# A pool of its own for the second layer's modulation with eight load tiles, the squares of the first norm through PSUM, and transfers for the keys and queries

## The chip, the cores and the metric

The kernel runs on one core of a Trainium2 chip. The engines are named as in the profile: PE (TensorE matmul; PEld is its weight load), DVE (VectorE), ACT (ScalarE), POOL (GpSimd) and SP (SyncE), whose queue issues every DMA of this kernel. The metric is the device time of one execution in microseconds.

## The reference

A small diffusion step of two layers on 128 context tokens and 1024 latent tokens of width 1024. Each layer has a token mixer and a convolutional FFN, both with a modulated RMS norm in front and a gated residual behind.

```python
mc = split(sc @ w_mod[i] + b_mod[i], 6); ml = split(sl @ w_mod[i] + b_mod[i], 6)   # modulation, 2 vectors
hc = rmsnorm(xc, norm_mix[i]) * (1 + mc[1]) + mc[0]       # rmsnorm: x * rsqrt(mean(x*x) + EPS) * g
# layer 0: q, k, v, p = h @ w_in; q, k normed per head; neighbourhood attention of 8 heads
#          (context keys in one softmax with the neighbourhood), pooling of p; concatenation @ w_out
# layer 1: conformer convolution module
xc = xc + mc[2] * yc
hc = rmsnorm(xc, norm_ffn[i]) * (1 + mc[4]) + mc[3]
xc = xc + mc[5] * conv_ffn(hc, ...)                       # @ w_in, conv of 3, silu(a) * g, @ w_out
```

## The kernel before, in words

Everything is feature-major: a tile has 128 features on the partitions and the 1154 columns of the tokens (128 context, a gap of 2, 1024 latent) on the free axis; the residual x is eight such tiles (k = 0 to 7). A float32 product is made of three products of a split pair: `hi` is the value rounded to fp32r (ACT), `lo` the rest (POOL or DVE), and PE does hi*hi, hi*lo, lo*hi.

The work in order of time:

- **The start** (`start0`, L457 to L530). SP loads constants, the eight x, the parameters, then 16 tiles of modulation weights (`mraw`, 512 KB each) with two weight tiles of V (`wraw`) between them. ACT squares each x into an SBUF tile (`sq`, tag `prob`, two buffers); PE sums each square over the partitions with 9 fp32 matmuls of one column (L484), 72 in all, into `ms`. DVE and POOL make the reciprocal root (`rsv`, `rsr`, L368 and L371), PE spreads it over the partitions (`rb`, L490), ACT copies it out (`rs`). The modulation comes in four quarters: eight matmuls (`modps`, L502), a copy (`modev`), four small matmuls (`modt`, L508), then `md` and `g` on DVE. DVE and ACT then make `hhi` and `hlo` of two k per quarter (L521, L524, L525), and PE starts the projection of V (`vps`, L606 to L609) with them.
- **The projections and the attention.** `project_qk` makes the queries and keys of a pair of heads. `split_half` (L664) prepares them for one head b of a pair: of 128 partitions, 64 (`own`) hold the rounded keys `ks` and the other 64 (`oth`) the same again, copied by DVE (L680); `km` gets the rest of the keys (POOL, L681); `qs` gets the rounded queries and, in `oth`, their rest (DVE, L687 and L688); `qm` gets a copy of the rounded queries from POOL (L691). `qm` and `km` are one tile each for head 0 and head 1 of a pair, used again by each of the four pairs, so there are eight halves. The scores (L697, L698) read all four.
- **The output projection** (`out_tiles`) in two parts of the tokens, then the FFN of layer 0, layer 1's convolution and FFN. Beside the output projection and layer 0's FFN, DVE computes the modulation of layer 1 (`mod_beside`, L309): for each of three groups, 32 loads of 128x512 (`mraw`, three buffers, 256 KB each) are multiplied by two scalars into eight accumulators (`modacc`, in tiles of the pool `cv`), and PE sums them over the partitions (L330). The generators are pulled at fixed places (`MS` = 4 loads per tile of the first output projection, `MO` and `MI` in the FFN).

Tiles come from pools with a fixed number of buffers, and the order of each engine's instructions is set by a list scheduler from priorities and modelled times. SP issues DMAs in its order too: one that waits holds up those behind it.

Of the kernel before, what the change touches and what calls it, by code (L numbers as in the profile page):

```python
# [9 lines left out]
F32 = mybir.dt.float32  # L10
F32R = mybir.dt.float32r
AF = mybir.ActivationFunctionType
ALU = mybir.AluOpType
# [6 lines left out]
P = 128  # L20
D = 1024
KT = D // P
# [4 lines left out]
T = L0 + NLAT  # L27
# [90 lines left out]
UW = 692  # L118
# [70 lines left out]
class Kern:  # L189
# [116 lines left out]
        self.mod_spread(l, m, ps, ev, *(last or (psp, tag)))  # L306
        yield

    def mod_beside(self, l, m, wp, ap, tag, ev):  # L309

        nc = self.nc
        accs = [ap.tile([P, UW], F32, tag=tag, name=self.nm("modacc"))[:, :512] for _ in range(8)]
        for k in range(KT):
            for u in range(2):
                for x in range(2):
                    rv = wp.tile([P, 512], F32, tag="mraw", name=self.nm("mraw"), bufs=3)
                    o = u * 1024 + x * 512
                    nc.sync.dma_start(rv, self.i["wmod"][l, m, k, :, o:o + 512])
                    for s in range(2):
                        acc, c = accs[4 * s + 2 * u + x], self.sc[:, k, s:s + 1]  # L320
                        if k == 0:
                            i = nc.vector.tensor_scalar(acc, rv, c, None, op0=ALU.mult)
                        else:
                            i = nc.vector.scalar_tensor_tensor(acc, rv, c, acc, op0=ALU.mult, op1=ALU.add)  # L324
                        self.tc.keep_in_program_order(i)
                    yield
        ps = self.psa.tile([P, 512], F32, tag="aux", name=self.nm("modps"))
        for s in range(2):
            for g in range(4):
                nc.tensor.matmul(ps[32 * g:32 * g + 32, :], self.one[:, 1 - s:33 - s], accs[4 * s + g],  # L330
                                 start=s == 0, stop=s == 1)
        yield
        self.mod_spread(l, m, ps, ev, self.psa, "aux")
        yield
# [122 lines left out]
    def start0(self, up, hp, ap, evac):  # L457


        nc = self.nc  # L460
        mm = nc.tensor.matmul
        xs, raws, wv = [], [], []
        nc.sync.dma_start(self.consts, self.i["consts"])
        for k in range(KT):
            x = up.tile([P, TS], F32, tag="u", name=f"x0_{k}")
            nc.sync.dma_start(x[:, :T], self.i["x"][k])
            xs.append(x[:, :T])
        nc.sync.dma_start(self.params, self.i["params"])
        nc.scalar.activation(self.sc[:, :, 0:2], self.par("cc").rearrange("p (a b) -> p a b", b=2), AF.Silu)
        nc.vector.tensor_scalar(self.qg8, self.par("qg", 0), DH ** -0.5, None, op0=ALU.mult)  # L470
        for i in range(16):
            raw = hp.tile([P, T], F32, tag="h", name=self.nm("mraw"))
            nc.sync.dma_start(raw[:, :1024], self.i["wmod0"][i])
            raws.append(raw)
            if i in (3, 7):
                wv.append(self.wload(self.i["wv"][i // 4]))
        st = [tok0(j) for j in range(9)]
        ms = self.psa.tile([P, 512], F32, tag="aux", name=self.nm("ms"))
        for k in range(KT):
            sq = ap.tile([P, 2, 640], F32, tag="prob", name=self.nm("sq"), bufs=2)  # L480
            sq = sq.rearrange("p a b -> p (a b)")[:, :T]
            nc.scalar.activation(sq, xs[k], AF.Square)
            for j, o in enumerate(st):
                mm(ms[:, j:j + 1], sq[:, o:o + P], self.cst("on"), start=k + j == 0, stop=k == KT - 1 and j == 8)  # L484
        r = self.rsqrt(ms[:, :9], 9)
        rb = self.psm.tile([P, 3, 512], F32, tag="mm3", name=self.nm("rb"))
        for j in range(9):
            c = 0 if j < 3 else j // 3
            n = L0 if j == 0 else P
            mm(rb[:, c, st[j] - CH[c][0]:st[j] - CH[c][0] + n],  # L490
               r[:, j:j + 1].to_broadcast([P, P]), self.cst("id")[:, :n], start=True, stop=True)
        rs = up.tile([P, TS], F32, tag="u", name=self.nm("rs"))
        for pv, sv in self.row3(rb, rs):
            nc.scalar.activation(sv, pv, AF.Copy)
        hhi, hlo = [], []

        def quarters():
            for j in range(4):
                ps = self.psa.tile([P, 512], F32, tag="aux", name=self.nm("modps"))
                for k in range(KT):  # L500
                    g = 32 * (k % 4)
                    mm(ps[g:g + 32, :], self.sc[:, k, :], raws[4 * j + k // 2][:, (k % 2) * 512:(k % 2) * 512 + 512],  # L502
                       start=k < 4, stop=k >= 4)
                ev = evac()
                nc.vector.tensor_copy(ev, ps)
                mt = self.psa.tile([P, 512], F32, tag="aux", name=self.nm("modt"))
                for x in range(4):
                    mm(mt[:, 2 * x:2 * x + 2], ev[:, x * P:(x + 1) * P], self.cst("sl2"), start=True, stop=True)  # L508
                md = self.cp.tile([P, 2, 2, 2], F32, name=self.nm("md"))
                nc.vector.tensor_tensor(md, mt[:, 0:8].rearrange("p (a k s) -> p a k s", a=2, k=2),  # L510
                                        self.par("bm0")[:, :16].rearrange("p (a k) -> p a k", a=2)
                                        [:, :, 2 * j:2 * j + 2, None].to_broadcast([P, 2, 2, 2]), op=ALU.add)
                g = self.cp.tile([P, 2, 2], F32, name=self.nm("g0"))
                nc.vector.scalar_tensor_tensor(g, md[:, 1], 1.0, self.par("nm0")[:, 2 * j:2 * j + 2, None]
                                               .to_broadcast([P, 2, 2]), op0=ALU.add, op1=ALU.mult)
                for x in range(2):
                    t = xs[2 * j + x]
                    hi = hp.tile([P, T], F32R, tag="h", name=self.nm("hhi"))
                    lo = hp.tile([P, T], F32R, tag="h", name=self.nm("hlo"))
                    for s, a, b in ((0, 0, L0), (1, L0, T)):  # L520
                        nc.vector.scalar_tensor_tensor(t[:, a:b], rs[:, a:b], g[:, x, s:s + 1], t[:, a:b],  # L521
                                                       op0=ALU.mult, op1=ALU.mult)
                    for s, a, b in ((0, 0, L0), (1, L0, T)):
                        nc.scalar.activation(hi[:, a:b], t[:, a:b], AF.Identity, bias=md[:, 0, x, s:s + 1], scale=1.0)  # L524
                        nc.vector.scalar_tensor_tensor(lo[:, a:b], t[:, a:b], md[:, 0, x, s:s + 1],  # L525
                                                       hi[:, a:b].bitcast(F32), op0=ALU.add, op1=ALU.subtract)
                    hhi.append(hi)
                    hlo.append(lo)
                yield
        return hhi, hlo, quarters(), wv  # L530
# [133 lines left out]
    def split_half(self, q, k, b, new, res):  # L664


        nc = self.nc
# [4 lines left out]
        def blk(t):  # L672
            return t.rearrange("p (g r c) -> p r g c", g=4, c=16)

        own = slice(64 * b, 64 * b + 64)
        oth = slice(64 - 64 * b, 128 - 64 * b)
        ks = new("ks")
        nc.scalar.activation(ks[own, :], k[own, :T], AF.Copy)
        yield
        nc.vector.tensor_copy(ks[oth, :], k[own, :T])  # L680
        nc.gpsimd.tensor_tensor(self.km[b][own, :], k[own, :T], ks[own, :].bitcast(F32), op=ALU.subtract)  # L681
        yield
        qs = new("qs")
# [4 lines left out]
        nc.vector.tensor_tensor(blk(qs[oth, L0:T]), lat(q[own, L0:T]), blk(qs[own, L0:T]).bitcast(F32),  # L688
                                op=ALU.subtract)
        for o, e in ((0, NCTX), (L0, T)):  # L690
            nc.gpsimd.tensor_copy(self.qm[b][own, o:e], qs[own, o:e])  # L691
        res[b] = (qs, ks)
        yield

# [547 lines left out]
    def trunk(self):  # L1242
        tc, nc, I, cp = self.tc, self.nc, self.i, self.cp
# [10 lines left out]
        with ExitStack() as st:  # L1254
            pool = lambda n, b, **kw: st.enter_context(tc.tile_pool(name=n, bufs=b, reuse_waits="tile", **kw))
# [7 lines left out]
            ft = pool("ft", 4, side="right")  # L1263
            self.fp = pool("fp", 3, side="right")
            hB = pool("hB", 16)
            nt = pool("nt", 3)
            sp = self.sp = pool("cv", 12)
            self.tw = 664
            xs = []
            for k in range(KT):  # L1270
# [8 lines left out]
            for part, Hc in ((OA, mkA()), (OB, mkB(OB.c0))):  # L1279
                Hc.order = order  # L1280
                tiles = {}
                for k in order:
# [5 lines left out]
                                            op=ALU.subtract)  # L1288
# [4 lines left out]
                if part is OA:  # L1293
                    for k in range(KT):
                        nc.sync.dma_start(xs[k], I["x"][k])
            mods = [self.mod_beside(1, m, nt, sp, "s", lambda: nt.tile([P, self.tw], F32, tag="ft", name=self.nm("modev")))
                    for m in range(3)]
            for _ in self.out_tiles(OA, I["woab"], cat[OA], xs, self.mod(0, 2), 0, 664, first=3):
                self.pull(mods, MS)
# [12 lines left out]
            for o in self.ffn(0, FA0, xs, HA, self.mod(0, 5), 0, 662, ft, None):  # L1312
                self.tick(MO if o else MI)
            self.flush(self.bg)


            gm1 = self.gain(1, 1, "nm1")
# [2 lines left out]
            accs = []  # L1320
# [30 lines left out]
            accs = []  # L1351
# [145 lines left out]
```

## Time and profile before

| | us |
|---|---|
| median of 3 runs | 2718.06 (2717.0 to 2720.67) |
| profiled execution | 2718.41 |
| its span | 2716.6 |
| PE busy | 2635.2 (97%) |
| DVE busy | 1605.9 (59%) |
| POOL busy | 1260.9 (46%) |
| ACT busy | 1122.9 (41%) |
| moved by DMA | 341.17 MB |

The span is what the profiler recorded; 1.8 us of the execution's own time lie around it. An engine counts as busy while an instruction is on it, also where that instruction waits inside for a port, and PE is busy too where it works at half its rate or on matmuls of one column. So a busy share says where there is no room left, not that the work there is needed.

### The profile page before, as it was taken

Reading aid. Unit: us, or ns where it says so; the run is one execution under the profiler, and the core shown is the slowest. Engines: PE = TensorE matmul, PEld = TensorE weight load, DVE = VectorE, ACT = ScalarE, POOL = GpSimd, SP = SyncE. Lnnn points to the kernel's source line nnn. Section 1 sums busy time; section 2 is a strip of 40 time slices with the busy share of each in tenths; the row PEclk is TensorE's granted clock in tenths of the full one; section 3 lists DMA queues with packets and bytes.
Section 4 is the critical chain, followed back from the end, with each engine's and each line's share of the span. In section 5 each row is a group of like instructions: output and inputs, shape, how many; then the busy total and the mean of one; then the engine's idle time right before and its main releaser. Section 6 shows DMA issues by size and latency. Waiting matters only on the chain.

```text
span 2716.6 us, 38806 instructions
## 1 busy us (share of the span) xinstructions
PE 2635.2 (97%) x15108; PEld 2379.8 (88%) x15108; DVE 1605.9 (59%) x2456; ACT 1122.9 (41%) x1743; POOL 1260.9 (46%) x752
## 2 busy tenths in 40 slices
PE   8999998889999999999999999999999999999999
PEld 6688887688999999988998789989999999888887
DVE  2236777575476757663997854369974334444444
ACT  3325766525422222245555363555324323433332
POOL 1323444146433232225555353699756544655553
PEclk9999998999999999999999999999999999999999
DMA  7622214364446555544434553232222222433232
GB/s 266 198 76 69 56 53 131 92 223 146 145 150 202 175 174 192 193 147 156 142 133 144 178 179 116 85 88 77 70 74 70 77 85 71 125 93 93 93 95 92
DMA packets 137815, 341.17 MB, mean 126 GB/s; under 512 B 45728, under 2 KB 50976, under 8 KB 137632
## 3 DMA queue, kind: packets, MB, share of 16 engines
q1 hardware_dynamic: 137632, 338.69, 38.8%
q8 instruction: 120, 1.97, 0.3%
q14 instruction: 63, 0.52, 0.1%
HBM read 291.97 MB, written 46.67 MB: 125 GB/s over the span
## 4 chain that ended last, share of the span: by engine, by line
PE 80%; DVE 12%; DMA 3%; ACT 3%; issue 1%; POOL 1%; SPq 0%; POOLq 0%; DVEq 0%; ACTq 0%
PE mm L264 14%; PE mm L266 14%; PE mm L268 14%; PE mn L264 7%; PE mn L266 7%; PE mn L268 7%; DVE modacc L324 2%; DVE dacc L992 2%; PE mm L454 2%; DVE x L437 2%; PE O L884 1%; PE ms L484 1%; PE tp L852 1%; PE qps L634 1%; PE qps L636 1%
## 5 line engine op out<-in xcount | busy, mean ns | idle before, releaser
L254 POOL TENSOR_TENSOR wlo<-wraw,whi 128x1024 fp32r<-128x1024 f32 x280 | 686.0, 2455 | 926.1 <-ACT whi L252 792.6
L252 ACT ACTIVATE whi<-wraw 128x1024 fp32r<-128x1024 f32 x348 | 364.7, 1057 | 770.4 <-PE mm L266 404.5
L264 PE MATMUL mm<-h,whi 128*128 128x332 f32 (+6 forms) x2208 | 559.0, 324 | 11.5 <-DVE x L437 11.5
L268 PE MATMUL mm<-h,wlo 128*128 128x332 f32 (+6 forms) x2208 | 560.5, 324 | 0.4 <-POOL wlo L254 0.3
L266 PE MATMUL mm<-h,whi 128*128 128x332 f32 (+6 forms) x2208 | 559.5, 324 | 0.0
L264 PEld LDWEIGHTS mm<-h,whi 128*128 128x128 f32 x2208 | 383.0, 189 | 25.9 <-issue 12.8
L268 PEld LDWEIGHTS mm<-h,wlo 128*128 128x128 f32 x2208 | 381.3, 189 | 12.4 <-POOL wlo L254 0.9
L266 PEld LDWEIGHTS mm<-h,whi 128*128 128x128 f32 x2208 | 380.0, 189 | 10.4
L992 DVE SCALAR_TENSOR_TENSOR dacc<-u,params,dacc 128x661 f32<-128x661 f32 (+1 forms) x344 | 285.4, 830 | 7.7
L437 DVE SCALAR_TENSOR_TENSOR x<-mm,mod,x 128x128 f32<-128x128 f32 (+7 forms) x408 | 210.4, 561 | 128.3 <-PE mm L268 126.4
L264 PE MATMUL mn<-h,whi 128*128 128x494 f32 (+1 forms) x672 | 262.6, 391 | 3.2 <-DVE x L437 3.2
L266 PE MATMUL mn<-h,whi 128*128 128x494 f32 (+1 forms) x672 | 262.2, 390 | 0.0
L268 PE MATMUL mn<-h,wlo 128*128 128x494 f32 (+1 forms) x672 | 260.6, 390 | 0.0
L1088 DVE SCALAR_TENSOR_TENSOR facc<-mm,params,facc 128x663 f32<-128x663 f32 (+3 forms) x92 | 82.1, 892 | 275.3 <-ACT facc L1087 275.2
L1088 DVE SCALAR_TENSOR_TENSOR facc<-mn,params,facc 128x493 f32<-128x493 f32 (+1 forms) x84 | 62.0, 738 | 219.2 <-ACT facc L1087 219.1
L264 PE MATMUL mm<-fh,whi 128*128 128x332 f32 (+2 forms) x720 | 172.0, 318 | 15.0 <-DVE x L437 13.1
L268 PE MATMUL mm<-fh,wlo 128*128 128x332 f32 (+2 forms) x720 | 170.2, 316 | 0.0
L266 PE MATMUL mm<-fl,whi 128*128 128x332 f32 (+2 forms) x720 | 170.0, 316 | 0.0
L974 POOL TENSOR_TENSOR acc<-acc,tap 128x508 f32<-128x508 f32 (+1 forms) x104 | 151.2, 1457 | 37.1 <-ACT tap L973 31.2
L324 DVE SCALAR_TENSOR_TENSOR modacc<-mraw,sc,modacc 128x512 f32<-128x512 f32 x168 | 158.4, 992 | 0.1
L1100 POOL TENSOR_TENSOR facc<-facc,facc 128x494 f32<-128x494 f32 (+2 forms) x66 | 91.2, 1381 | 144.9 <-DVE facc L1090 136.8
L437 DVE SCALAR_TENSOR_TENSOR x<-mn,mod,x 128x510 f32<-128x510 f32 (+1 forms) x168 | 120.5, 737 | 63.7 <-PE mn L268 62.9
(227 smaller groups left out, 4520.5 us busy)
## 6 DMA issues: line engine op xcount, KB each, us to landing
wraw<-in_fi_dram SPq DMA_DIRECT2D x176, 512.0 KB
wraw<-in_fo_dram SPq DMA_DIRECT2D x88, 512.0 KB
mraw<-in_wmod_dram SPq DMA_DIRECT2D x48, 512.0 KB
mraw<-in_wmod_dram SPq DMA_DIRECT2D x96, 256.0 KB
wraw<-in_pw_dram SPq DMA_DIRECT2D x48, 512.0 KB
lowi<-wlo SPq DMA_DIRECT2D x44, 512.0 KB
wlo<-lowi SPq DMA_DIRECT2D x44, 512.0 KB
lowo<-wlo SPq DMA_DIRECT2D x22, 512.0 KB
```

The source lines that it names most:

```text
L252: nc.scalar.activation(hi, raw, AF.Copy)
L254: (eng or nc.gpsimd).tensor_tensor(lo, raw, hi.bitcast(F32), op=ALU.subtract)
L264: mm(pv, whi, xhi[:, a:b], start=start, stop=False)
L266: mm(pv, whi, xlo[:, a:b], start=False, stop=False)
L268: mm(pv, wlo, xhi[:, a:b], start=False, stop=stop)
L324: i = nc.vector.scalar_tensor_tensor(acc, rv, c, acc, op0=ALU.mult, op1=ALU.add)
L437: nc.vector.scalar_tensor_tensor(xd[:, a:b], pv, gate[:, d, st:st + 1], xd[:, a:b], op0=ALU.mult, op1=ALU.add)
L454: mm(ps[:, c, :n], w[:, s], x[k][:, o:o + n], start=a, stop=b)
L974: nc.gpsimd.tensor_tensor(acc[:, :n], acc[:, :n], p[:, :n], op=ALU.add)
L992: nc.vector.scalar_tensor_tensor(acc[:, :n] if t == NCK - 1 else pacc, u[:, t:t + n], wk(i, t), acc[:, :n] if t == side else pacc, op0=ALU ...
L1088: nc.vector.scalar_tensor_tensor(acc[:, 1:W], part.ps(ps, 0, W - 1), w(0), acc[:, 1:W], op0=ALU.mult, op1=ALU.add)
L1100: (nc.gpsimd if side or part.n == 1 else nc.vector).tensor_tensor(a[:, :W], a[:, :W], g[:, :W], op=ALU.mult)
```

## The change

Four edits:

- In `start0` the squares of k = 1 to 7 go to PSUM tiles (`mm3`), and DVE adds them to the first square in SBUF (L485 of the new kernel); PE then sums over the partitions once, with 9 matmuls instead of 72 (L488).
- In `split_half` the copy of the rounded keys is a DMA from `own` to `oth` instead of a DVE cast, and the copies of the rounded queries to `qm` are DMAs instead of POOL copies. Each of the eight halves gets one DMA for the keys (64 partitions of 1154 columns) and two for the queries (128 and 1024 columns), 24 in all, issued by SP.
- `mod_beside` has a pool `mp` with eight buffers for the loads and eight for the accumulators.
- That pool is closed after layer 0's first FFN part, and the pool `cv` is opened behind it in its place.

```diff
-        accs = [ap.tile([P, UW], F32, tag=tag, name=self.nm("modacc"))[:, :512] for _ in range(8)]
+        accs = [mp.tile([P, 512], F32, tag="macc", name=self.nm("modacc")) for _ in range(8)]
...
-                    rv = wp.tile([P, 512], F32, tag="mraw", name=self.nm("mraw"), bufs=3)
+                    rv = mp.tile([P, 512], F32, tag="mraw", name=self.nm("mraw"))
...
-        ms = self.psa.tile([P, 512], F32, tag="aux", name=self.nm("ms"))
-        for k in range(KT):
-            sq = ap.tile([P, 2, 640], F32, tag="prob", name=self.nm("sq"), bufs=2)
+        acc = ap.tile([P, 2, 640], F32, tag="prob", name=self.nm("sq"), bufs=2)
+        acc = acc.rearrange("p a b -> p (a b)")[:, :T]
+        nc.scalar.activation(acc, xs[0], AF.Square)
+        for k in range(1, KT):
+            sq = self.psm.tile([P, 3, 512], F32, tag="mm3", name=self.nm("sq"))
             sq = sq.rearrange("p a b -> p (a b)")[:, :T]
             nc.scalar.activation(sq, xs[k], AF.Square)
-            for j, o in enumerate(st):
-                mm(ms[:, j:j + 1], sq[:, o:o + P], self.cst("on"), start=k + j == 0, stop=k == KT - 1 and j == 8)
+            nc.vector.tensor_tensor(acc, acc, sq, op=ALU.add)
+        ms = self.psa.tile([P, 512], F32, tag="aux", name=self.nm("ms"))
+        for j, o in enumerate(st):
+            mm(ms[:, j:j + 1], acc[:, o:o + P], self.cst("on"), start=True, stop=True)
...
-        nc.vector.tensor_copy(ks[oth, :], k[own, :T])
+        nc.sync.dma_start(ks[oth, :].bitcast(F32), ks[own, :].bitcast(F32))
...
-            nc.gpsimd.tensor_copy(self.qm[b][own, o:e], qs[own, o:e])
+            nc.sync.dma_start(self.qm[b][own, o:e].bitcast(F32), qs[own, o:e].bitcast(F32))
...
-            sp = self.sp = pool("cv", 12)
+            beside = ExitStack()
+            mp = beside.enter_context(tc.tile_pool(name="mp", bufs=8, reuse_waits="tile"))
...
-            mods = [self.mod_beside(1, m, nt, sp, "s", lambda: nt.tile([P, self.tw], F32, tag="ft", name=self.nm("modev")))
+            mods = [self.mod_beside(1, m, mp, lambda: nt.tile([P, self.tw], F32, tag="ft", name=self.nm("modev")))
...
+            beside.close()
+            sp = pool("cv", 12)
```

What PE does first in the program, before (`ms` is the sum of the squares, `modps` a quarter of the modulation, `vps` the projection of V; x9 folds nine matmuls):

```order
L484 MATMUL ms_233<-consts,sq_234 128x1 x9
L484 MATMUL ms_233<-consts,sq_245 128x1 x9
L484 MATMUL ms_233<-consts,sq_256 128x1 x9
L484 MATMUL ms_233<-consts,sq_267 128x1 x9
L502 MATMUL modps_339<-mraw_197,sc 32x512 x2
L484 MATMUL ms_233<-consts,sq_278 128x1 x9
L484 MATMUL ms_233<-consts,sq_289 128x1 x9
L502 MATMUL modps_339<-mraw_199,sc 32x512 x2
L502 MATMUL modps_339<-mraw_201,sc 32x512 x2
L502 MATMUL modps_339<-mraw_203,sc 32x512
L484 MATMUL ms_233<-consts,sq_300 128x1 x9
L484 MATMUL ms_233<-consts,sq_311 128x1 x9
```

The same place of the changed kernel:

```order
L488 MATMUL ms_256<-consts,sq_233 128x1 x9
L506 MATMUL modps_283<-mraw_197,sc 32x512 x2
L506 MATMUL modps_283<-mraw_199,sc 32x512 x2
L506 MATMUL modps_283<-mraw_201,sc 32x512 x2
L506 MATMUL modps_283<-mraw_203,sc 32x512 x2
L494 MATMUL rb_270<-consts,rsr_267 128x130
L494 MATMUL rb_270<-consts,rsr_267 128x128 x8
L512 MATMUL modt_294<-consts,modev_292 128x2 x4
L506 MATMUL modps_325<-mraw_207,sc 32x512 x2
L506 MATMUL modps_325<-mraw_209,sc 32x512 x2
L506 MATMUL modps_325<-mraw_211,sc 32x512 x2
L506 MATMUL modps_325<-mraw_213,sc 32x512 x2
```

Eight groups of `ms` became one, `rb` moved ahead of the second quarter, and the rows that follow are the first of `vps`.

DVE at the same place of the changed kernel, behind its memsets (`sq_233` is the sum of the squares; `qg` waits for the parameters; `wlo_322` is the first weight tile of V):

```order
L485 TENSOR_TENSOR sq_233<-sq_233,sq_235 128x1154
L485 TENSOR_TENSOR sq_233<-sq_233,sq_238 128x1154
L485 TENSOR_TENSOR sq_233<-sq_233,sq_241 128x1154
L485 TENSOR_TENSOR sq_233<-sq_233,sq_244 128x1154
L485 TENSOR_TENSOR sq_233<-sq_233,sq_247 128x1154
L485 TENSOR_TENSOR sq_233<-sq_233,sq_250 128x1154
L470 TENSOR_SCALAR qg_150<-params 128x1
L485 TENSOR_TENSOR sq_233<-sq_233,sq_253 128x1154
L368 TENSOR_SCALAR rsv_266<-ms_256 128x9
```

Before, `qg`, two weight tiles of V and then `rsv` stood here; the seven adds are new.

SP at the last pair of heads, in the changed kernel (`vr` are rows of V, `tr` the bias, `mraw` the modulation weights; the last two figures of a row are the tile's shape):

```order
L750 DMA tr_4610<-in_rpb_dram 16x16x48 x8
L789 DMA vr_4710<-vd 128x1x64
L684 DMA ks_4231<-ks_4231 64x1154
L695 DMA qm_155<-qs_4310 64x128
L695 DMA qm_155<-qs_4310 64x1024
L684 DMA ks_4543<-ks_4543 64x1154
L695 DMA qm_156<-qs_4547 64x128
L789 DMA vr_4710<-vd 128x1x64
L695 DMA qm_156<-qs_4547 64x1024
L789 DMA vr_4710<-vd 128x1x64 x2
L300 DMA mraw_4742<-in_wmod_dram 128x1024
L300 DMA mraw_4790<-in_wmod_dram 128x1024
```

The six transfers of the two halves stand between loads of `vr` and ahead of the loads of `mraw`; before, `vr` and `mraw` followed `tr` directly.

## Rows read from the trace of the kernel before

**Rows 1.** The page: busy time, and the chain that ended last by engine.

```profile
PE 2635.2 (97%) x15108; PEld 2379.8 (88%) x15108; DVE 1605.9 (59%) x2456; ACT 1122.9 (41%) x1743; POOL 1260.9 (46%) x752
PE 80%; DVE 12%; DMA 3%; ACT 3%; issue 1%; POOL 1%; SPq 0%; POOLq 0%; DVEq 0%; ACTq 0%
```

**Rows 2.** Windows: stretch; PE, PEld, DVE, ACT, POOL busy; granted clock; DMA share; GB/s.

```profile
0.00:50.00 50.00, 42.80 (x184) 34.23 (x184) 5.08 (x13) 15.24 (x16) 5.36 (x12) 1.00 0.91 336
```

**Rows 3.** Groups by line and form, 0 to 110 us: busy, mean ns; idle before.

```profile
L484 PE MATMUL ms<-consts,sq 128*128 128x1 f32 x144 | 31.2, 352 | 6.4 <-ACT sq L482 6.4
```

**Rows 4.** Timeline of the start: start, us, engine, line, operation; idle before, releaser.

```profile
17.54 0.15 DVE L470 TENSOR_SCALAR qg<-params 128x1 f32<-128x1 f32 x1 [16.21 <-DMA params<-in_params_dram]
...
23.94 1.06 ACT L252 ACTIVATE whi<-wraw 128x1024 fp32r<-128x1024 f32 x1 [0.76 <-DMA wraw<-in_wv_dram]
...
31.64 1.17 ACT L482 ACTIVATE sq<-x 128x1154 f32<-128x1154 f32 x1 [2.67 <-PE ms L484]
...
43.23 1.81 POOL L371 TENSOR_TENSOR rsr<-rsv,mhalf 128x9 f32<-128x9 f32 x1 [41.83 <-DVE rsv L368]
...
45.50 1.87 PE L508 MATMUL modt<-consts,modev 128*128 128x2 f32 x8 [0.78 <-DVE modev L505]
...
47.29 3.37 PE L502 MATMUL modps<-mraw,sc 128*32 128x512 f32 x16
...
50.60 2.27 PE L490 MATMUL rb<-consts,rsr 128*128 128x130 f32 x18
...
56.66 0.50 PE L606 MATMUL vps<-whi,hhi 128*128 128x512 f32 x1 [0.49 <-ACT hhi L524]
```

**Rows 5.** Window of the start while the loads run.

```profile
15.00:20.00 5.00, 5.00 (x25) 5.00 (x25) 0.15 (x1) 2.91 (x4) 0.00 (x0) 1.00 1.02 411
```

**Rows 6.** Timeline of DVE: an addition in SBUF, a product with PSUM.

```profile
604.55 0.84 DVE L406 TENSOR_TENSOR sq<-sq,sq 128x664 f32<-128x664 f32 x1
...
638.83 1.60 DVE L419 TENSOR_TENSOR nt<-mm,x 128x664 f32<-128x664 f32 x2 [1.86 <-PE mm L392]
```

**Rows 7.** Lines 680 and 691: duration ns min/median/max, first and last start.

```profile
L680 DVE CAST ks<-qk x8: 758/2008/3146, 219.9 to 456.3; 64x1154 fp32r<-64x1154 f32 x8
L691 POOL CAST qm<-qs x16: 353/930/2088, 231.8 to 464.6; 64x128 fp32r<-64x128 f32 x8, 64x1024 fp32r<-64x1024 f32 x8
```

**Rows 8.** Windows around the halves of the second and fourth pair.

```profile
290.00:320.00 30.00, 26.37 (x190) 23.29 (x188) 26.21 (x53) 20.49 (x51) 18.83 (x17) 1.00 0.19 43
450.00:480.00 30.00, 23.37 (x126) 12.40 (x124) 24.44 (x41) 16.33 (x40) 18.42 (x13) 0.77 0.68 206
```

**Rows 9.** Waits of PE, 200 to 550 us: us in total, times, longest.

```profile
PE O L879 <- DVE ptl L857: 7.0, 5, 2.8
PE O L884 <- DVE ptl L857: 6.3, 6, 2.3
```

**Rows 10.** Timeline of the fourth pair's halves.

```profile
455.47 3.95 DVE L680 CAST ks<-qk 64x1154 fp32r<-64x1154 f32 x2
...
461.88 1.01 PE L697 MATMUL S<-ks,qs 128*128 128x384 f32 x2 [0.46 <-DVE qs L688]
```

**Rows 11.** Chain in order of time: start, us, two transfers that ended a wait.

```profile
297.30 2.25 DMA vr<-vd
...
539.03 3.96 DMA cat<-ao
```

**Rows 12.** Waits of SP's queue, 200 to 550 us: us in total, times, longest.

```profile
SPq L898 <- DVE ao L895: 32.2, 2, 27.0
```

**Rows 13.** Window of the output projection.

```profile
600.00:630.00 30.00, 21.34 (x89) 17.72 (x89) 29.92 (x34) 5.94 (x7) 12.86 (x4) 0.90 0.52 160
```

**Rows 14.** Timeline of the output projection, DVE and POOL.

```profile
599.58 5.05 DVE L324 SCALAR_TENSOR_TENSOR modacc<-mraw,sc,modacc 128x512 f32<-128x512 f32 x4
...
608.90 2.73 DVE L324 SCALAR_TENSOR_TENSOR modacc<-mraw,sc,modacc 128x512 f32<-128x512 f32 x4
...
601.54 2.53 POOL L254 TENSOR_TENSOR wlo<-wraw,whi 128x1024 fp32r<-128x1024 f32 x1 [6.79 <-ACT whi L252]
```

More of the change, by code (lines that the diff above doesn't have):

```diff
@@ L307, in mod_group, with mod_beside @@
         yield
-    def mod_beside(self, l, m, wp, ap, tag, ev):
+    def mod_beside(self, l, m, mp, ev):
         nc = self.nc
-        accs = [ap.tile([P, UW], F32, tag=tag, name=self.nm("modacc"))[:, :512] for _ in range(8)]
+        accs = [mp.tile([P, 512], F32, tag="macc", name=self.nm("modacc")) for _ in range(8)]
         for k in range(KT):
```

## The prediction

> **What bounds the kernel.** I read the page first: PE is busy for 2635.2 of 2716.6 us and holds 80% of the chain that ended last [rows 1]. So only two things can gain: PE's idle time, 81.4 us, and PE time spent on work that isn't needed. The windows show where both lie. Behind the output projection the change takes no work from PE. The first 50 us look well filled, 42.80 us [rows 2], but the groups by form say on what: 144 records (two per fp32 matmul) of the one-column sum `ms` take 31.2 us [rows 3]. That is the second kind. The timeline of the start shows what waits for it: POOL begins the root only at 43.23, and the projection of V streams from 56.66 [rows 4]. The other idle time lies in the attention, where DVE is late for PE [rows 8, 9], and in the output projection, where DVE is busy for 29.92 of 30 us [rows 13].
>
> **The start.** Removed are 63 of the 72 matmuls of `ms`; at 31.2/144 = 0.217 us per record that is 27.3 us of PE. Added are seven additions on DVE. The trace has no addition of 1154 columns with one operand in PSUM; an SBUF addition of 664 columns took 0.84 us, a product with PSUM 0.80 [rows 6], so by columns 1.39 to 1.46, and I take 1.4. They lie beside the loads of x, all but the last. The new chain, step by step:
> - Parameters land by 17.5 [rows 4]; they stand right behind the last x in the queue, 387 KB, which at 411 GB/s [rows 5] is 0.9 us, so the last x lands by 16.6. Square 1.2, last addition 1.4 (it comes behind `qg`, 17.7): 19.2.
> - Nine matmuls of `ms`, 18 records: 3.9, to 23.1. `rsv` and the root, 1.81 and some 0.3 [rows 4]: 25.2.
> - Beside it the first quarter `modps`. Its loads stand just ahead of the V tile that landed by 23.94, so they are there; 3.37 at the slow rate of this early row [rows 4], 23.1 to 26.5. The root is covered by it.
> - `rb` now goes next, 2.27, to 28.8; then `modt` 1.87, to 30.7. Before, both quarters' small steps were done ahead of `rb`, now `md` and `g` come behind it. From the start of `rb` to the stream of V before: 56.66 - 50.60 = 6.1. With the 2 us of `modt` on the path: 26.5 + 6.1 + 2 = 34.6.
> - The second quarter stands ahead of V on PE. Its four loads of 512 KB end 5.1 us (2.1 MB at 411 GB/s) behind 23.94, at 29, so it runs from 30.7 to 34.1 and hides beside the above.
> So V streams from about 34.6, 22 us earlier. Behind it every stage waits for PE or for a buffer that PE frees, so I let the 22 us through. Bounds: if PE is still slow for the first of V, or a load is 3 us later, 17; if `rb` goes with the root at 25.2 and the small steps overlap, 24. **-22 us.**
>
> **Keys and queries.** Removed: eight casts on DVE, median 2.0 us and 0.76 to 3.15, some 16 us, and 16 copies on POOL, median 0.93, some 15 us [rows 7]. Added: 24 transfers on SP's queue. DVE's part matters only where PE waits for DVE: 290 to 320 (3.6 us of PE idle) and 450 to 480 (6.6 idle; mean granted clock 0.77, so PE, having fallen idle, was at 1.2 GHz for part of it) [rows 8]; PE's waits for DVE's `ptl` sum to 13.3 us over the attention [rows 9]. In the fourth pair the two casts hold DVE for 3.95 us [rows 10], and `ptl` stands behind them. A transfer of 64x1154 within SBUF isn't in the trace. The nearest are a small read of V from DRAM, 2.25 us, and a store of 128x1154, 3.96 [rows 11]; the size lies between, I take 3.1. In the fourth pair, if ACT begins to round where the casts begin, 455.47, and takes 1.2 us for the keys and 1.2 for the queries, as for a square of that width [rows 4], the keys land at 459.8 and the queries at 461.0: ahead of the scores at 461.88 [rows 10], which waited for DVE's `qs`, and that has 2 us less in front of it. What is late next is `qm`. Queued behind a waiting transfer on SP are loads of `vr`, bias and modulation weights; `vr` has two buffers, so a load has a unit of work to spare. Best case all of both windows' idle time, 10.3, and (1 - 0.77) x 23.37 = 5 of slow clock, -15; worst, each of eight halves about 1 us later, half of the distance from a cast's 2.0 to 3.96, +8. I take half of the idle time, 5, and 1 for the clock: **-6 us.**
>
> The Trainium skill speaks against these transfers: "DMA: Bandwidth & Descriptors", section on the anatomy of one DMA, fits about 2.0 us fixed plus the bytes over 436 GB/s, though for the other kind of queue. As an estimate that is 2.7 us for 295 KB, longer than the cast it replaces by 0.7 us at the median; eight in series would make this term +5 and the time 2701. No row here shows such a transfer, and the sum doesn't use it.
>
> **The pool of the modulation.** The loads run up to eight tiles ahead instead of three; DVE's instructions are the same. In the output projection four `modacc` took 2.73 us at 608.90 and 5.05 at 599.58, and in the second case POOL's `wlo` ran from 601.54 for 2.53 [rows 14]. The excess, 2.3 us, is about that instruction. So DVE is held up by POOL, not by a load, and more load tiles give nothing. If it were the loads, all of PE's idle time there, 8.7 us [rows 13], would go. The eight accumulators instead of 12 shared tiles make the second group wait for the sums of the first, which PE gets a step earlier. `cv` opens behind work that ended long before. Five loads instead of three stand ahead of the last load of `cat`, which waits for its store anyway, 3.96 us [rows 11]: hidden. **0, bounds -9 and +1.**
>
> The rule on DVE and POOL in "SBUF — State Buffer", section "Who interferes with whom", is that the pair of ports they share is locked for the whole instruction. By that rule this term is 0; by waits for loads it would be -9. The two rows agree with the rule to 0.2 us.
>
> **Sum.** -22 - 6 + 0 = -28 on the profiled execution's 2718.41: 2690.4. The median of the runs is 0.35 lower: 2690.
>
> **Rivals.**
> - Transfers eat their own gain: each is late by half a microsecond to one, attention 0 to +8, start as above. 2696 to 2704. For: no slack at 461.88, 0.46 us waited there [rows 10]. Against: POOL's copies stood behind `km` and were later than ACT.
> - The loads set the start after all: V can't run before the last quarter's weights, 13 tiles or 6.8 MB behind 23.94, that is 16.6 us, so 40.5, and 6.1 of steps: 46.6, and 10 us are left. 2708 without the attention's gain, 2702 with it. Against: quarters are used two k at a time.
> - The casts and the load tiles were worth more: attention -15, output projection up to -9. 2672 to 2681. For: 13.3 us of waits [rows 9]; against: the two rows of POOL.
> - Slower: SP's queue in order. A transfer at its head waits for ACT or for the last scores that read `qm`, and `vr`, weights and bias behind it come late; SP has already stood for 27.0 us at one store [rows 12]. If each half delays PE by a full transfer, 3.96 x 8 = 31.7, less 22: 2728. It decides from 22/8 = 2.8 us per half. Against: the buffers of `vr`.
>
> **How the numbers follow.** Forecast (2683 to 2696) 0.55; transfers eat their gain 0.2; loads set the start 0.1; worth more 0.1; slower 0.05. The range for 8 in 10, with the bounds of the sum, 2675 to 2708. A measurement can tell 0.2% here, 5.4 us: all but the last case are faster by more, and I take 0.04 off for those that reach the bound: faster 0.91, same 0.05, slower 0.04.
>
> **What would show it.** After: `ms` x18 in one piece at about 19 to 23, V streaming from 33 to 37; 31.2 us of `ms` down to 4. In the attention PE's idle time at 270 to 300 and 425 to 455 smaller, no `ks` on DVE. Per output tile the same 9 us, `modacc` still 5 with `wlo`. Wrong if V starts behind 46, if PE waits for `ks` or `qm` transfers for over 8 us in all, or if `modacc` runs without the excess.

## The result, and the profile after

The changed kernel takes 2697.35 us (median of four runs, 2696.8 to 2698.98), the kernel before 2718.15 beside it: ratio 0.9925, 95% interval 0.9913 to 0.9937, 20.8 us less. The forecast was 2690, its range 2675 to 2708; the time lies 7 us above the forecast and just outside the likeliest case's own 2683 to 2696. The profiled execution's span falls from 2716.6 to 2694.8, by 21.8. Stations on the way show where. `vps` is the projection of V; "V streams" is its row behind PE's last wait ahead of V, as in [rows 4], and the next station is the start of the last `vps` of its first pass. `tp` are the transposes of the attention, with their first and last start:

| | before | after | earlier by |
|---|---|---|---|
| V streams | 56.66 | 32.09 | 24.6 |
| last `vps` of V's first pass | 115.8 | 105.1 | 10.7 |
| first `tp` | 243.8 | 232.6 | 11.2 |
| last `tp` | 534.7 | 514.6 | 20.1 |
| end of the span | 2716.6 | 2694.8 | 21.8 |

So the start gained more than was forecast, 14 us of it were gone 73 us later, and the attention gave 9. The page of the profile first, beside [rows 1]: 29.8 us less PE, and PE's share of the chain up from 80 to 82%.

```profile
PE 2605.4 (97%) x14982; PEld 2352.9 (87%) x14982; DVE 1597.6 (59%) x2455; ACT 1124.1 (42%) x1743; POOL 1244.9 (46%) x736
...
PE 82%; DVE 10%; ACT 2%; issue 2%; DMA 2%; POOL 1%; SPq 0%; POOLq 0%; DVEq 0%; ACTq 0%
```

The group of `ms` after, by line and form (busy, mean ns; idle before), answers to [rows 3]: 31.2 us have become 4.0.

```profile
L488 PE MATMUL ms<-consts,sq 128*128 128x1 f32 x18 | 4.0, 353 | 18.2 <-DVE sq L485 18.2
```

The timeline of the start after (start, us, engine, operation; idle before, releaser) answers to [rows 4]. Read it as the forecast's list of steps: last addition, `ms` in one piece, the first quarter with the root (POOL) beside it, `rb`, `modt`, the second quarter, V.

```profile
16.80 1.36 DVE L485 TENSOR_TENSOR sq<-sq,sq 128x1154 f32<-128x1154 f32 x1
...
18.21 4.00 PE L488 MATMUL ms<-consts,sq 128*128 128x1 f32 x18 [18.21 <-DVE sq L485]
...
22.14 3.61 PE L506 MATMUL modps<-mraw,sc 128*32 128x512 f32 x16
...
22.57 1.81 POOL L371 TENSOR_TENSOR rsr<-rsv,mhalf 128x9 f32<-128x9 f32 x1 [21.18 <-DVE rsv L368]
...
25.68 2.27 PE L494 MATMUL rb<-consts,rsr 128*128 128x130 f32 x18
...
27.79 0.95 PE L512 MATMUL modt<-consts,modev 128*128 128x2 f32 x8
28.68 1.92 PE L506 MATMUL modps<-mraw,sc 128*32 128x512 f32 x16
...
32.09 0.50 PE L610 MATMUL vps<-whi,hhi 128*128 128x512 f32 x1 [0.83 <-ACT hhi L528]
```

**Where 14 us went.** V's first pass, from the first `vps` to the last, is 60.4 us long before (55.4 to 115.8) and 74.6 after (30.5 to 105.1). The groups of PE in that stretch say what else ran in it. Before:

```profile
L609 PE MATMUL vps<-whi,hlo 128*128 128x512 f32 x72 | 19.8, 397 | 0.0
L303 PE MATMUL modps<-mraw,sc 128*32 128x512 f32 x24 | 5.3, 605 | 0.0
L502 PE MATMUL modps<-mraw,sc 128*32 128x512 f32 x20 | 2.5, 597 | 0.0
L508 PE MATMUL modt<-consts,modev 128*128 128x2 f32 x16 | 1.9, 241 | 0.0
```

After:

```profile
L613 PE MATMUL vps<-whi,hlo 128*128 128x512 f32 x72 | 20.4, 403 | 3.6 <-DVE hlo L529 3.6
L303 PE MATMUL modps<-mraw,sc 128*32 128x512 f32 x32 | 8.2, 633 | 0.4 <-DMA mraw<-in_wmod_dram 0.4
L506 PE MATMUL modps<-mraw,sc 128*32 128x512 f32 x36 | 5.5, 599 | 0.0
L512 PE MATMUL modt<-consts,modev 128*128 128x2 f32 x24 | 3.6, 272 | 0.0
```

The quarters' products (L502, L506) and `modt`, which had run ahead of V, now run inside it: 3.0 and 1.7 us more; 2.9 more are an early part of the next modulation (L303). The three kinds of `vps` together take 79.8 instead of 77.3, and PE is idle for 4.8 instead of 0.5. That sums to 14.4. The idle part and the slow part have one place, as two windows after show (PE busy first; granted clock third from the end):

```profile
60.00:65.00 5.00, 2.84 (x11) 2.35 (x11) 4.16 (x4) 0.00 (x0) 1.02 (x1) 0.81 0.53 157
65.00:70.00 5.00, 5.00 (x13) 2.94 (x14) 3.69 (x8) 2.17 (x4) 0.00 (x0) 0.50 0.00 0
```

PE fell idle, and for the next 5 us the granted clock was 0.50, the level of 1.2 GHz. The timelines of SP, DVE, ACT, POOL and PE ahead of it, after:

```profile
20.27 9.22 SPq L473 DMA_DIRECT2D mraw<-in_wmod_dram  x8
...
31.72 11.35 SPq L750 DMA_DIRECT2D tr<-in_rpb_dram  x8
...
45.02 0.85 SPq L236 DMA_DIRECT2D wraw<-in_wv_dram  x2
...
51.29 5.15 DVE L525 SCALAR_TENSOR_TENSOR x<-rs,g,x 128x130 f32<-128x130 f32 x4
...
51.76 1.06 ACT L252 ACTIVATE whi<-wraw 128x1024 fp32r<-128x1024 f32 x1 [4.75 <-DMA wraw<-in_wv_dram]
...
52.90 2.45 POOL L254 TENSOR_TENSOR wlo<-wraw,whi 128x1024 fp32r<-128x1024 f32 x1 [4.33 <-DVE x L525]
...
57.22 1.60 DVE L773 CAST ck<-craw 64x256 fp32r<-64x256 f32 x2
...
62.16 1.69 PE L613 MATMUL vps<-whi,hlo 128*128 128x512 f32 x5 [3.58 <-DVE hlo L529]
```

SP stands for 11.35 us at the eight issues of `tr`, the bias rows of the first head, first read at 183, and only then issues the third weight tile of V, which is needed next. Most of it is waiting, as SP's waits show (us in total, times, longest):

```profile
SPq L750 <- DMA mraw<-in_wmod_dram: 9.3, 8, 2.1
```

Each issue waits until the load eight places ahead of it has landed, and those are `mraw` of 512 KB; a `tr` has 48 KB. Once the third weight tile is issued, ACT waits 4.75 us for it. POOL's `wlo` then falls beside DVE's four `x`, which take 5.15 us here and 3.01 in the other quarters; the casts of `ck` behind them take 1.60 instead of 0.59, and PE waits 3.58 for the `hlo` that comes last. Before, the same eight issues stood at the same time, and V began behind them:

```profile
32.18 10.31 SPq L746 DMA_DIRECT2D tr<-in_rpb_dram  x8
...
43.82 0.99 SPq L236 DMA_DIRECT2D wraw<-in_wv_dram  x2
```

**Attention and output projection.** PE's waits after, 200 to 550 us, answer to [rows 9]: 13.3 us for `ptl` have become 9.9, and PE waits once for a transfer of the keys.

```profile
PE O L888 <- DVE ptl L861: 7.2, 7, 2.2
PE O L883 <- DVE ptl L861: 2.7, 3, 1.6
...
PE C L701 <- DMA ks<-ks: 1.5, 1, 1.5
```

The windows around the halves of the second and fourth pair, at the same place of the attention, answer to [rows 8]: PE's idle time in both is 7.7 us instead of 10.3, and the clock in the second 0.89 instead of 0.77. From the first `tp` to the last, PE is idle for 16.2 us instead of 23.5 and busy for 265.8 instead of 267.4: most of the 8.9 us is idle time.

```profile
280.00:310.00 30.00, 26.75 (x193) 24.08 (x192) 25.01 (x54) 20.88 (x55) 13.81 (x12) 1.00 0.36 84
440.00:470.00 30.00, 25.53 (x150) 16.37 (x149) 21.86 (x49) 18.73 (x48) 11.37 (x8) 0.89 0.71 190
```

DVE's groups in the attention, before:

```profile
L680 DVE CAST ks<-qk 64x1154 fp32r<-64x1154 f32 x7 | 15.0, 2137 | 0.3
...
L688 DVE TENSOR_TENSOR qs<-qk,qs 64x1024 fp32r<-64x1024 f32 x7 | 10.4, 1484 | 0.1
L687 DVE TENSOR_TENSOR qs<-qk,qs 64x128 fp32r<-64x128 f32 x7 | 9.3, 1330 | 1.9 <-ACT qs L684 1.8
```

After:

```profile
L691 DVE TENSOR_TENSOR qs<-qk,qs 64x128 fp32r<-64x128 f32 x7 | 18.0, 2568 | 1.3 <-ACT qs L688 1.0
...
L692 DVE TENSOR_TENSOR qs<-qk,qs 64x1024 fp32r<-64x1024 f32 x7 | 8.5, 1214 | 0.0
```

The casts took 15.0 us, but DVE is only 8.2 us freer (34.7 to 26.5): the subtraction of 64x128, 0.28 us where it stands alone, now falls beside POOL's `km` of 2.67 and takes as long as that. The Trainium skill ("SBUF — State Buffer", "Who interferes with whom") has DVE and POOL share one pair of ports under an exclusive lock; the trace agrees.

DVE's `modacc` in the output projection, beside POOL, answers to [rows 14]:

```profile
587.27 8.66 DVE L324 SCALAR_TENSOR_TENSOR modacc<-mraw,sc,modacc 128x512 f32<-128x512 f32 x8
...
589.23 2.85 POOL L254 TENSOR_TENSOR wlo<-wraw,whi 128x1024 fp32r<-128x1024 f32 x1 [0.60 <-ACT whi L252]
...
597.56 2.72 DVE L324 SCALAR_TENSOR_TENSOR modacc<-mraw,sc,modacc 128x512 f32<-128x512 f32 x4
```

Eight take 3.2 us more than twice four: the excess beside `wlo` is still there with eight load tiles. It isn't there each time: of four groups of eight in this stretch two have it (7.53 us at 571.12 and this one) and two do not (5.38 at 580.27, 5.37 at 597.56); beside these two it is POOL's `wlo` that is longer, 5.38 and 6.43 instead of 2.4.

### The profile page after: what moved, and what is told of

It is laid out like the page before. It is cut to its first block, busy times and chain, and to the rows that moved or that the text cites. A ratio compares the mean times of both kernels' runs of the same rounds, so it can differ in the third digit from the quotient of the medians.

```text
span 2694.8 us, 38615 instructions
## 1 busy us (share of the span) xinstructions
PE 2605.4 (97%) x14982; PEld 2352.9 (87%) x14982; DVE 1597.6 (59%) x2455; ACT 1124.1 (42%) x1743; POOL 1244.9 (46%) x736
## 4 chain that ended last, share of the span: by engine, by line
PE 82%; DVE 10%; ACT 2%; issue 2%; DMA 2%; POOL 1%; SPq 0%; POOLq 0%; DVEq 0%; ACTq 0%
PE mm L264 15%; PE mm L268 15%; PE mm L266 15%; PE mn L264 8%; PE mn L266 8%; PE mn L268 8%; PE mm L454 2%; DVE modacc L324 2%; DVE x L437 2%; PE O L888 2%; DVE dacc L996 1%; PE tp L856 1%; PE qps L638 1%; PE qps L639 1%; PE qps L640 1%
## 5 line engine op out<-in xcount | busy, mean ns | idle before, releaser
L266 PEld LDWEIGHTS mm<-h,whi 128*128 128x128 f32 x2208 | 379.7, 189 | 10.4
L1107 ACT ACTIVATE fh<-facc 128x664 fp32r<-128x664 f32 (+3 forms) x88 | 60.2, 684 | 227.5 <-POOL facc L1104 140.1
```

The costliest lines, as they stand in the source:

```text
L266: mm(pv, whi, xlo[:, a:b], start=False, stop=False)
L1107: nc.scalar.activation(hi[:, :W], a[:, :W], AF.Copy)
```

## The experiments

All were timed beside the kernel before, whose medians were 2718.44, 2717.80 and 2717.96 in the three series. The stations are of the one profiled execution of each; "attention" is from the first to the last `tp`.

| | median us | ratio, 95% | V's first pass ends | first `tp` | attention |
|---|---|---|---|---|---|
| before | 2718.15 | 1 | 115.8 | 243.8 | 290.9 |
| changed | 2697.35 | 0.9925 (0.9913 to 0.9937) | 105.1 | 232.6 | 282.0 |
| e1 squares alone | 2703.72 | 0.9953 (0.9941 to 0.9965) | 106.6 | 233.9 | 283.7 |
| e2 transfers alone | 2707.12 | 0.9965 (0.9953 to 0.9978) | 117.5 | 243.7 | 280.9 |
| e3 pool alone | 2717.45 | 0.9999 (0.9990 to 1.0008) | 114.7 | 242.8 | 290.4 |
| e4 changed, `tr` and `craw` held | 2691.00 | 0.9898 (0.9885 to 0.9912) | 100.5 | 225.7 | 282.9 |
| e5 before, both held | 2714.74 | 0.9984 (0.9976 to 0.9993) | 115.0 | 246.4 | 286.3 |
| e6 changed, `tr` held | 2690.36 | 0.9892 (0.9879 to 0.9906) | 98.6 | 223.5 | 284.4 |
| e7 changed, keys alone by transfer | 2708.05 | 0.9962 (0.9949 to 0.9974) | 107.5 | 235.9 | 288.8 |
| e8 changed, queries alone by transfer | 2697.61 | 0.9924 (0.9910 to 0.9937) | 106.4 | 234.6 | 281.1 |
| e9 changed, squares in SBUF | 2691.32 | 0.9903 (0.9888 to 0.9918) | 106.5 | 233.0 | 280.5 |
| e10 changed, three load tiles | 2699.61 | 0.9944 (0.9931 to 0.9958) | 105.4 | 236.8 | 282.1 |
| e11 changed, `tr` held, no transfers | 2689.47 | 0.9905 (0.9891 to 0.9919) | 99.9 | 226.2 | 284.6 |
| e12 changed, `tr` held, queries alone | 2695.08 | 0.9919 (0.9906 to 0.9933) | 100.2 | 225.2 | 289.5 |

**e1, the squares alone**: the diff of `start0` above, on the kernel before.

> The kernel before with the edit of the squares alone. Theory: V streams at about 32 as in the changed kernel, but some 14 us of the 24.6 are given back inside the projection of V, because the weights of V and the third quarter come no earlier than the loads in front of them; so the end is 10 to 12 us earlier: 2707, 2704 to 2710. Rival, the give-back came from the transfers on SP's queue or from the pool: with the squares alone the whole gain of the start reaches the end, 2694 to 2698.

V's first pass ends at 106.6 and the first `tp` is 9.9 us earlier: the give-back belongs to the start itself, and the rival falls. Unforeseen, the attention is 7.2 us shorter, though nothing in it was edited, and the time lies just below the theory's 2704.

**e2, the transfers alone**, on the kernel before:

```diff
-        nc.vector.tensor_copy(ks[oth, :], k[own, :T])
+        nc.sync.dma_start(ks[oth, :].bitcast(F32), ks[own, :].bitcast(F32))
-            nc.gpsimd.tensor_copy(self.qm[b][own, o:e], qs[own, o:e])
+            nc.sync.dma_start(self.qm[b][own, o:e].bitcast(F32), qs[own, o:e].bitcast(F32))
```

> The kernel before with the keys and queries moved by transfers, nothing else. Theory: the attention gains as in the changed kernel, 9 us, of which PE's waits for ptl are some 3: 2709, 2706 to 2712. Rival, the 9 us came from another order of the instructions in the changed kernel and not from the transfers: 2715 to 2721. Rival, SP's queue in order: over 2722.

As the theory said, 10.0 us of attention. Yet e1 and e2 give 7.2 and 10.0, and the changed kernel, which has both, 8.9: they don't add up, so a cost per transfer or cast can't be all.

**e3, the pool alone**: the diff of `mod_beside` and of its pools above, on the kernel before.

> The kernel before with the pool of the modulation alone, eight load tiles. Theory: DVE is held by POOL in the output projection and not by a load, so no difference: 2718, 2715 to 2720. Rival, the pool is what gains the 2 us behind the attention: 2714 to 2716. The rule of loads: 2709.

No difference that can be measured. In the traces the stretch from the first `ms` of the output projection's norm (L380) to the end is 2093.2 to 2093.4 us in the four kernels without the pool (before, e1, e2, e5) and 2088.3 to 2091.2 in eight of the nine with eight load tiles (the ninth is e11 with 2094.2, whose profiled execution lies 6.3 us above its median): some 3 us that the times don't resolve, and one execution can move this stretch by more.

**e4, `tr` and `craw` held**, on the changed kernel. A one-column copy makes the first loads wait for `vctx`, written at the end of V's first pass:

```diff
+        if h == 0:
+            nc.scalar.activation(tr[:, 0, 0:1], self.vctx[:, 0, 0, 0:1].bitcast(F32), AF.Copy)
         for r in range(8):
...
+        if pr == 0:
+            nc.scalar.activation(raw[:, 0, 0:1], self.vctx[:, 0, 0, 0:1].bitcast(F32), AF.Copy)
+            nc.scalar.activation(raw[:, 1, 0:1], self.vctx[:, 0, 0, 0:1].bitcast(F32), AF.Copy)
```

> The changed kernel, with the first bias rows tr and the first craw made to wait for vctx (a one-column copy into their tiles ahead of the load), so that the weights of V stand ahead of them in SP's queue. Theory: the 11.35 us that SP spends on the eight tr issues hold back V's third and fourth weights; without them 8 to 12 of the 14 us come back: 2685 to 2690, and V's first group ends at 93 to 97 instead of 105. Rival, the order of DVE and PE (the third quarter's modt late on PE) holds V: 2694 to 2698, first group still ends behind 101. Rival, what was held comes too late for the attention: over 2698.

6.4 us come back, 6.9 at the first `tp`: what stood ahead in the queue was the cause, but the theory had put 8 to 12 on it, and V's first pass ends at 100.5, not by 97. What stays in V's first pass, 68.3 us against 60.4, is mostly PE work that moved in: there the groups L506, L512 and L303 come to 15.7 against 9.7 before, 6.0 more, and PE's idle time to 1.9.

**e5, the same hold on the kernel before.**

> The kernel before with the same hold on the first tr and craw, nothing of the change. Theory: before, V begins at 56 and the issues of tr lie beside the sums of ms, so nothing waits for what they hold back: 2718, 2714 to 2721. Rival, the hold is worth its 6 us by itself, whatever the start does: 2709 to 2713.

V's first pass ends 0.8 us earlier and the first `tp` comes 2.6 later: in the start the hold is worth nothing there, as the theory said. In the trace the gain lies in the attention, 4.6 us shorter, in which nothing was edited.

**e6, `tr` alone held** (the first two lines of e4).

> The changed kernel with the first tr alone held, craw as it was. Theory: it is the 11.35 us of SP's queue that the tr issues take: as with both held, 2689 to 2693. Rival, it is the two casts of ck on DVE (0.59 and 1.60 us) and the work on craw by ACT and POOL in front of the third quarter: 2695 to 2698.

As with both held; so the issues of `tr`, not the casts of `ck`, are what held V. The timeline of e6: V's third weight tile is issued at 36.65, ACT has it at 45.16, and the casts of `ck` are still there. The third quarter's `modt`, the rival of e4, was not what held V either: it runs at 50.78 here and ran at 49.90 in the changed kernel.

```profile
36.65 1.59 SPq L236 DMA_DIRECT2D wraw<-in_wv_dram  x2
...
45.16 1.06 ACT L252 ACTIVATE whi<-wraw 128x1024 fp32r<-128x1024 f32 x1 [1.65 <-DMA wraw<-in_wv_dram]
...
45.69 0.70 DVE L775 CAST ck<-craw 64x256 fp32r<-64x256 f32 x2
```

Its windows where the changed kernel stood still; PE is full and the clock at 2.4 GHz:

```profile
60.00:65.00 5.00, 5.00 (x27) 4.26 (x26) 1.91 (x5) 0.41 (x1) 0.00 (x0) 1.00 0.27 98
65.00:70.00 5.00, 5.00 (x26) 3.12 (x25) 5.00 (x6) 3.44 (x4) 2.57 (x1) 1.00 0.45 131
```

e6 beats both kernels: its interval, 0.9879 to 0.9906, lies below that of the changed kernel.

**e7 and e8, one kind of transfer each**, on the changed kernel. e7 puts POOL's copies of the queries back, e8 DVE's casts of the keys:

```diff
# e7
-            nc.sync.dma_start(self.qm[b][own, o:e].bitcast(F32), qs[own, o:e].bitcast(F32))
+            nc.gpsimd.tensor_copy(self.qm[b][own, o:e], qs[own, o:e])
# e8
-        nc.sync.dma_start(ks[oth, :].bitcast(F32), ks[own, :].bitcast(F32))
+        nc.vector.tensor_copy(ks[oth, :], k[own, :T])
```

> The changed kernel with the copies of the queries back on POOL: only the keys go by transfer. Theory: DVE's part is the casts of the keys, POOL's copies are off the path: 2697, 2695 to 2699. Rival, POOL is what DVE collides with, so the queries' copies count: 2700 to 2704.

> The changed kernel with the casts of the keys back on DVE: only the queries go by transfer. Theory: the gain of the transfers is in the keys, so it is lost: 2700 to 2703. Rival, the squares alone have already shortened the attention by 7 us (first to last tp 290.9 before, 283.7 with the squares alone), so the transfers add nothing there: 2696 to 2698.

Both theories fall. e8 has the time of its rival, but not for the rival's reason: if the transfers added nothing, e7 would have lost nothing. With the casts of the keys back (e8) nothing is lost; with the keys alone (e7) the attention is 288.8 and the time 10.7 us longer than the changed kernel's. Part of e7's loss is one place, which no edit touched: PE waits 3.1 us for one `ptl`, which DVE makes behind casts of `ck` and two `prob` (368.08 to 370.32), and is then at 1.2 GHz. Two windows of e7:

```profile
365.00:370.00 5.00, 2.48 (x25) 1.93 (x23) 4.27 (x12) 3.00 (x9) 2.72 (x5) 0.97 0.10 28
370.00:375.00 5.00, 3.94 (x16) 2.44 (x18) 2.70 (x7) 0.95 (x2) 0.00 (x0) 0.50 0.06 13
```

**e9, the squares in SBUF**, on the changed kernel:

```diff
-            sq = self.psm.tile([P, 3, 512], F32, tag="mm3", name=self.nm("sq"))
+            sq = ap.tile([P, 2, 640], F32, tag="prob", name=self.nm("sq"), bufs=2)
```

> The changed kernel with the squares of the tiles 1 to 7 in SBUF (the second prob tile, free again behind each addition) and not in PSUM. Theory: what gains is the seven additions in place of 63 matmuls; ACT, waiting for the one tile, makes a square and DVE adds it one behind the other, some 1.2 us later at the end: 2698, 2696 to 2700, V streaming at 32 to 34. Rival, PSUM is what makes the chain short (two tiles of squares in flight, additions at 1.36 us): V streams behind 36 and the end is 2702 or more.

Timeline and duration rows of e9:

```profile
25.65 4.00 PE L488 MATMUL ms<-consts,sq 128*128 128x1 f32 x18 [25.65 <-DVE sq L485]
...
40.52 0.53 PE L610 MATMUL vps<-whi,hhi 128*128 128x512 f32 x1 [0.79 <-ACT hhi L528]
```

```profile
L613 PE MATMUL vps<-whi,hlo x72: 389/396/503, 43.0 to 106.5; 128*128 128x512 f32 x72
```

ACT and DVE take turns on the one free tile, 2.6 us per square, so `ms` is 7.4 us later and V streams 8.4 later, as the rival had it. But V's first pass ends at 106.5 against 105.1, the first `tp` comes 0.4 later, and the time is no longer. This is the plainest proof that V's beginning didn't set its end in the changed kernel: to begin 8.4 us later costs 1.4 at the end. In e9 the third weight tile is issued at 43.43, much as in the changed kernel (45.02), and PE, which begins V later, waits for no `hlo`: the first pass is 67.5 us long, and PE is idle in it for 1.9 instead of 4.8. (That the kernel is 6 us faster is not told apart: the intervals overlap.)

**e10, three load tiles**, on the changed kernel: `bufs=3` for `mraw` in the pool.

> The changed kernel with three load tiles in the modulation's own pool in place of eight. Theory: DVE in the output projection is held by POOL, so the depth is worth nothing, and the 2 to 3 us that the four kernels with the pool show between the first trunk ms and the end come from the accumulators' own tiles: 2697, 2695 to 2699. Rival, the loads run ahead and save the 2 to 3 us: 2699.5 to 2701.

2.3 us longer, as the rival had it, but the intervals overlap, and the profiled execution lies 6.3 us above its median. Whether the depth is worth 2 us stays open. The trace is of use for another question. Up to the last `tp` PE, DVE, ACT and POOL have the same instructions in the same order as in the changed kernel, and the attention has the same length, 282.1 and 282.0. But the first `tp` comes 4.2 us later, so that station alone moves by as much with nothing changed ahead of it.

**e11, `tr` held and no transfers** (e6 with both edits of e2 undone).

> The changed kernel with tr held and the keys and queries back on DVE and POOL: squares, pool and hold, no transfers. Theory: the transfers shorten the attention (first to last tp) from 284 to 291 without the queries' transfers to 281 to 284 with them, so it is longer here, 286 to 290, and the end is 2693 to 2698. Rival, the length of the attention is the planner's luck and not the transfers: 281 to 284 here too, and 2689 to 2692.

The rival holds: 2689.47 without any transfer, 2690.36 with all, and an attention of 284.6 against 284.4. Here they are worth nothing that can be measured. The durations of `tp` in e11, with first and last start:

```profile
L858 PE MATMUL tp<-consts,prob x328: 270/273/435, 226.2 to 510.8; 128*128 128x128 f32 x164
```

**e12, `tr` held, queries alone by transfer** (e6 with the edit of e8).

> The changed kernel with tr held and the keys cast on DVE: squares, pool, hold and the queries' transfers. Theory: the keys' transfers are worth nothing, so as with all of them, 2690, 2688 to 2692. Rival, the keys' transfers were needed and only hidden by the late start: 2694 or more.

2695.08, on the rival's side, but e11, which has no transfer of keys either, is no longer (5.6 us shorter, though the intervals overlap); so the keys' transfers are not what e12 lacks. The attention of e12, 289.5 us, stands beside 281.1 in e8, which differs only in the loads at the start. PE's idle time there is 20.5 against 19.2; the rest is busy time, 269.0 against 261.9, at a granted clock of 0.94 against 0.98.

## Why the prediction was right, and where it was wrong

**The chain of the start was right, by its steps.** V was to stream at 34.6 and streams at 32.09. The addition was taken as 1.4 and took 1.36; `ms` 3.9, took 4.00; the root hid beside the first quarter; `rb` took its 2.27. The steps behind `rb` were taken too long: the forecast used rows from ahead of it, 1.87 for `modt` and 3.37 for the second quarter, which took 0.95 and 1.92.

**"So I let the 22 us through" failed**, with the sentence before it, that every stage behind waits for PE or for a buffer that PE frees. Of the 24.6 us gained, 10.7 are left at the end of V's first pass (10.4 in e10) and 11.2 at the first `tp`. Two things were left out. The queue of SP: the argument looked at loads ahead of V's beginning, not at what stood ahead of V's third weight tile; e6 shows that this cost 7.0 us by the end, 6.5 at the end of V's first pass. That pass is 67.2 to 68.6 us long in the four kernels with `tr` held (e4, e6, e11, e12) and 74.6 to 75.1 in the five that begin V as early without the hold (changed, e1, e7, e8, e10). And PE work that had filled PE's waiting ahead of V: 4.7 us of quarters and `modt` had to be done inside V. The rival "loads set the start after all" had the size, 10 us left, but named the wrong loads: the last quarter's modulation weights, which nobody waited for.

**The keys and queries: a gain of 9 where 6 was forecast, but not shown to be theirs.** The step "`ptl` stands behind the casts" was wrong in its size: half of the casts' 15.0 us came back as the subtraction beside `km`. The windows of the halves did gain, 2.6 us of idle time and about as much of slow clock, but the transfers can't be shown to have shortened the attention: its length is 283.7, 284.6, 286.3, 290.4 and 290.9 in the five kernels without them, 281.1, 288.8 and 289.5 in the three with one kind, 280.5 to 284.4 in the six with both. e5 changes it by 4.6 us through a load at 31 us. As two pairs of kernels show, the order of the instructions sets it, and not the chance of one execution: e3 has the order of the kernel before on PE, DVE, ACT and POOL up to the last `tp`, and 290.4 us beside 290.9; e10 has the changed kernel's, and 282.1 beside 282.0. The scheduler sets the order anew with every edit at the start or in the attention, and that moves this stage by some 10 us. With both transfers it was never above 284.4, so a few microseconds may be theirs; e11 against e6 says none. What in an order makes 281 or 290 stays open. The slower rival did not come: PE waits 1.5 us in all for the keys and nothing for the queries.

**The pool: right within its bounds.** The excess beside `wlo` is still there in two of the four groups. The 3 us that the traces show were not foreseen, and the times do not show them.

**The sum.** -11.2 for the start, -8.9 in the attention, -1.7 behind it: -21.8, against -22, -6 and 0. The first term was twice what it turned out to be, and the other two made up for part of it: that the time lies in the range is in part luck. It also lies among the 2696 to 2704 of the rival "transfers eat their own gain", but not in its way, which had the start give 22 and the attention 0 to +8. With `tr` held the time falls by 27.4 us, about the -28 of the sum, because the first term then arrives nearly whole: the first `tp` of e6 comes 20.3 us earlier than before.

## What to carry to other kernels

When a stage is moved up, go through each queue it needs from its new beginning on and ask what stands ahead of its next load there, not of its first: what was issued early because nobody was waiting now stands in the way. Count the places that it takes in the queue, not only its bytes. Where a scheduler sets the order anew, a change of 5 us in a stage that wasn't edited proves nothing about the edit; undo the part under two different plans before giving it a price. And an engine that is relieved of one instruction may only meet the next one at the same port.

## What was not expected of the hardware

- A small load took as long a turn in SP's queue as a large one. SP's issues in this kernel use eight semaphores in turn, and in this stretch each waits until the load eight places ahead of it has landed. Eight `mraw` of 512 KB took 9.22 us in this way and the eight `tr` of 48 KB behind them 11.35, though the issue of a `tr` itself lasts 0.31 to 0.64 us and that of a `wraw` of 512 KB 0.33 (55.38). At 244.64, with one large load in front, seven `tr` take 3.28 us together. While the `tr` held the eight places, the transfers ran short: 398 GB/s at 35 to 40 us, 101 at 40 to 45; e6 has 404 and 355.
- The addition of 1154 columns took 1.36 us with one operand in PSUM and 1.36 with both in SBUF (e9): PSUM cost DVE nothing here, it gave ACT a second tile to write.
- Where `modacc` and POOL's `wlo` meet in the output projection after, either can be the one that is held up: DVE's eight by 2.2 and 3.2 us, or `wlo`, 2.4 us alone, with 5.38 and 6.43.
